# Experts of two MoE layers put in order of their token counts on the chip, the small ones four abreast

## The chip, the cores and the metric
The kernel runs on one core of a Trainium2 chip. The metric is device time in microseconds (us), from the launch's start to the end of its last instruction. TensorE is written PE (its weight loads PEld), VectorE DVE, ScalarE ACT, GpSimd POOL, SyncE SP. SP issues nearly all DMAs. Everything is float32 or a pair of fp32r values, high and low half, unless said otherwise.

## The reference
Two transformer blocks over 512 tokens of width 1024. Each block ends in a two-level mixture of experts (MoE) with 32 experts, in 4 groups of 8. A token takes its best group, and in that the best two experts, so 1024 assignments go to 32 experts, 32 on average. The experts of block 1 have a hidden width F of 512, those of block 2 one of 256. In short:

```
grp_p, grp_idx = top_k(softmax(x @ w_grp + b_grp), 1)
in_grp = (x @ w_exp + b_exp).reshape(T, 4, 8)[arange(T), grp_idx[:, 0]]
top_l, top_i = top_k(in_grp, 2)
comb = grp_p * softmax(top_l)
y = zeros(T, 1024)
for (t, e, w) in assignments:          # e = grp_idx * 8 + top_i
    y[t] += w * ((silu(x[t] @ w1[e]) * (x[t] @ w3[e])) @ w2[e])
```

## The kernel before
The MoE layers (MoE1 in block 1, MoE2 in block 2) are two objects of one class, `Moe`. The router (`Route`) leaves in `rt` the rank of each token within its expert (L404; 0 where the token isn't the expert's) and in `wl` its weight, as high and low half (L433, L434). The 32 experts form 16 pairs. A pair has 128 slots, 64 for each expert; two pairs are gathered together as a unit, so there are 8 units.

For a unit, `onehot` (L451) compares `rt` with the slot numbers, and `gather_k` (L457) multiplies the normalized tokens (stationary, 128x128) by that matrix: 64 matmuls of 256 columns bring the tokens of 256 slots to the partitions. `slot_weights` (L464) brings their weights. For a pair, `gateup` multiplies gate and up (L643): the slots of each expert are a stationary of 64 columns, the weights are moved in 512 columns, and the experts j = 0 and 1 of the pair alternate, in the two halves of the array. `spread` (L631) transposes the one-hot matrix. `finish` transposes the product (L662), multiplies by the down weights (L673, again two abreast), scales by the modulation row and splits into halves (ACT `yh`, POOL `yl`), and sends the rows back to the tokens with 16 matmuls of 512 columns (`back`, L688), which DVE adds to the sum (L694). The down part of pair p runs amid the gate and up part of pair p+1 (`mid`).

Weights are streamed by SP (L566) into slots of 1 MB that rotate: 15 in MoE1, 8 in MoE2. A slot is free when the matmuls that read it are done. In MoE1 a pair is 12 tiles: 8 gate and up tiles as 128 partitions x 4 rows x 512 (each row of 2 KB a piece of its own in DRAM), 4 down tiles as 128 x 2 x 1024 (4 KB). In MoE2 it is 4 gate-up tiles, of two DMAs each, in pieces of 1 KB, and 2 down tiles. The list `jobs` sets SP's order: gate tiles of p, down tiles of p-1, up tiles of p. 15 tiles of MoE1 are sent for before its first matmul.

An expert with more than 64 tokens would need a further pass: `passes` (L519 to L524) works out their number `nex` from the largest rank, every engine reads it (L717), and a loop (L720) runs so often. In the runs shown it is 0. The order of instructions on each engine comes from a scheduler that interleaves them by its own estimate of times; around the router it is written by hand.

Of the kernel before, what the change touches and what calls it, by code (L numbers as in the profile page):

```python
# [20 lines left out]
P = 128  # L21
T = 512
TB = 4
# [4 lines left out]
NPAIR = 16  # L28
# [30 lines left out]
C_N = 664  # L59
# [9 lines left out]
def _constants():  # L69
# [14 lines left out]
    c[:, C_THR + 7] = 1e9  # L84
    e = np.zeros((33, RL), np.float32)
# [12 lines left out]


# [54 lines left out]
def body(tc, I, out, dbg=None):  # L154
# [15 lines left out]
    with top:  # L170
# [179 lines left out]
        class Route:  # L350
# [57 lines left out]

            def weights(self, a, b):
# [39 lines left out]
        def onehot(d, pm, n):  # L449
            w = [P, pm.shape[1], n, CAP]  # L450
            V.tensor_tensor(d.rearrange("p t (e s) -> p t e s", e=n), pm.unsqueeze(3).to_broadcast(w),  # L451
                            cst[:, C_IO64:C_IO64 + CAP].unsqueeze(1).unsqueeze(1).to_broadcast(w), op=ALU.is_equal)
# [7 lines left out]
        def slot_weights(d, wlx, o, n, pl):  # L460
            wsl = tl(pl, [P, 2], tag="wsl", bufs=2)
            for pp in range(n // 2):
                for tb in range(TB):
                    PE.matmul(o[:, 4 * pp:4 * pp + 4], d[:, tb, P * pp:P * pp + P],  # L464
                              wlx[:, tb, 2 * pp:2 * pp + 2, :].rearrange("p e l -> p (e l)"),
                              start=tb == 0, stop=tb == TB - 1)
            for j in range(2):
                hf = slice(CAP * j, CAP * j + CAP)
                V.tensor_reduce(wsl[hf, 0:n // 2], o[hf, 0:2 * n].rearrange("p (a j l) -> p a j l", j=2, l=2)[:, :, j, :],
                                axis=AX.X, op=ALU.add)  # L470
            return wsl
# [24 lines left out]
        class Lead:  # L496
# [18 lines left out]
            def passes(self, bank):  # L515
                pm = tl(rp, [P, 1], tag="pm", bufs=1)
                th = tl(rp, [1, 8], tag="th", bufs=1)
                o = bank("tr")
                yield lambda: V.tensor_reduce(pm, rt.rearrange("p t e -> p (t e)"), axis=AX.X, op=ALU.max)  # L519
                PE.transpose(o[0:1, 0:P], pm, ident)  # L520
                yield lambda: V.tensor_reduce(pm[0:1], o[0:1, 0:P], axis=AX.X, op=ALU.max)
                yield lambda: V.tensor_scalar(th, cst[0:1, C_THR:C_THR + 8], pm[0:1], None, op0=ALU.is_le)
                yield lambda: V.tensor_reduce(pm[0:1], th, axis=AX.X, op=ALU.add)
                yield lambda: V.tensor_copy(nex[0:1, 0:1], pm[0:1])  # L524

            def slots(self, bank):
                return self.d, self.xT, slot_weights(self.d, wl, bank("tr"), 4, rp)


        class Moe:  # L530
            def __init__(self, w1, w3, w2, F, wpool, npre, more=0):
                self.w = [w.rearrange("(q b) d f -> q b d f", b=4) for w in (w1, w3, w2)]
                self.F, self.FC = F, F // P
                self.wpool, self.more = wpool, more
                js = [self.thunks(self.static(p_), wpool, p_) for p_ in range(NPAIR)]
                nd = self.FC
                self.upto = []
                self.jobs = []
                for p_ in range(NPAIR):
                    self.jobs += js[p_][0:4]  # L540
                    if p_:
                        self.jobs += js[p_ - 1][-nd:]
                    self.jobs += js[p_][4:-nd]
                    self.upto.append(len(self.jobs))
                self.jobs += js[-1][-nd:]
# [4 lines left out]
            def static(self, p_):  # L550
                return lambda i, j: self.w[i][p_ // 2, 2 * (p_ % 2) + j]
# [6 lines left out]
            def thunks(self, get, wpool, key, half=1):  # L558
                def kview(ap):
                    return ap.rearrange("(k p) f -> p k f", p=P)  # L560

# [9 lines left out]
                kg, kd = 4 // half, max(2 // half, 1)  # L571
                if F == 512:
                    for i, nm in enumerate("gu"):
                        for s_ in range(KC // kg):
                            for j in range(2):
                                out_.append(mk(nm, j, s_, [P, kg, F], [
                                    (lambda t: t, lambda i=i, j=j, s_=s_: kview(get(i, j))[:, kg * s_:kg * s_ + kg, :])]))
                else:
                    for s_ in range(KC // kg):
                        for j in range(2):  # L580
                            out_.append(mk("gu", j, s_, [P, kg, 2, F], [
                                (lambda t, i=i: t[:, :, i, :], lambda i=i, j=j, s_=s_: kview(get(i, j))[:, kg * s_:kg * s_ + kg, :])
                                for i in range(2)]))
                if half > 1:
                    for s_ in range(self.FC):
                        for n in range(2):
                            for j in range(2):
# [3 lines left out]
                for s_ in range(self.FC // kd):  # L591
                    for j in range(2):
# [4 lines left out]
            def run(self, hs, acc, grow, side, lead, keep, area):  # L597
# [3 lines left out]
                with es:  # L601
# [8 lines left out]
                    def gather(pmx, wlx, pl, n, ar):  # L610
                        w = n * CAP
                        d = ar[0]()
                        onehot(d, pmx, n)
                        xT = ar[1]()
# [6 lines left out]
                        return d, xT, slot_weights(d, wlx, bk("m"), n, rp if n == 4 else pl)  # L621

                    def gateup(ga, pp, ws, key, half=1, last=False, mid=None):
# [14 lines left out]
                        for i in range(F // 256):  # L638
                            for k in range(KC):
                                for j in range(2):  # L640
# [11 lines left out]
                    def finish(st, ws, key, half=1, le=G, last=False):  # L652
# [15 lines left out]
                        for k in range(FC):  # L668
                            for n in range(2):
                                for j in range(2):  # L670
                                    w = ws[key, "d", j, (k, n)][:, 0] if half > 1 else \
                                        ws[key, "d", j, k // 2][:, k % 2, 512 * n:512 * n + 512]
                                    PE.matmul(os_[n][CAP * j:CAP * j + CAP], gT[:, k, CAP * j:CAP * j + CAP], w,  # L673
# [40 lines left out]
                    with ExitStack() as ls:  # L714
# [4 lines left out]
                        V.tensor_copy(cur, rt)  # L719
                        with tc.For_i(0, n, 1) as it:  # L720
# [8 lines left out]
                            with tc.For_i(0, NQUAD, 1) as iq:  # L729
# [6 lines left out]
                                for pp in range(2):  # L736
                                    gl = gather(pm4[:, :, 2 * pp:2 * pp + 2], wl4[:, :, 2 * pp:2 * pp + 2, :], lw, 2, local(lw, 2 * CAP))
# [19 lines left out]
                    held = NPAIR - (1 if big_ else NE2)  # L757

                    def down(st, p_):
                        cm = finish(st, self.tiles, p_, le=G if p_ + 1 < NPAIR else V, last=p_ >= held)  # L760
# [5 lines left out]
                    for p_ in range(NPAIR):  # L766
# [1365 lines left out]
```

## Time and profile before

| | |
|---|---|
| median of 3 runs | 2041.03 us (2038.62 to 2044.96) |
| profiled execution | 2044.01 us, span 2042.2 us |
| MoE1 (stretch 854 to 1409 us) | 555 us, PE busy 534.34 us, DMA 344 GB/s |
| between the MoEs (1409 to 1687) | 278 us, PE busy 242.60 us, DMA 91 GB/s |
| MoE2 (1687 to 2021) | 334 us, PE busy 332.18 us, DMA 277 GB/s |

The stretches are read off the timeline, from the first gate matmul of a MoE to its last combine. Matmuls are pipelined, so a group's busy time counts overlap once within the group, and several groups can be busy at once; the time from the start of one matmul to the start of the next says what a matmul costs PE. A `SPq` row is a DMA issue and the time it waited, not the transfer.

### The profile page before, as it was taken

To read this page: it belongs to the slowest core of one execution; us is meant where nothing else is said; L and a number is where in the kernel's file an instruction comes from. 1 tells how busy PE (TensorE), PEld (TensorE's weight loads), DVE (VectorE), ACT (ScalarE), POOL (GpSimd) and SP (SyncE) were. 2 spreads that over 40 slices of the span, in tenths; PEclk is the share of its full clock that TensorE was granted. 3 is DMA by queue.
4 is the path that set the end of the run, shared out by engine and by line. 5 is a ranking of instruction groups with operands and counts; after the bars stand their busy time and mean duration, and the time that the engine had idled before them with its cause. 6 is when DMAs were issued, how large, how long until landed. Compare 5 with 4: busy or idle time off the path is not lost. (4 is left out here: it accounts for less than half of the span.)

```text
span 2042.2 us, 25610 instructions
## 1 busy us (share of the span) xinstructions
PE 1877.7 (92%) x10105; PEld 1231.2 (60%) x10105; DVE 939.5 (46%) x1667; ACT 652.4 (32%) x1076; POOL 463.6 (23%) x372
## 2 busy tenths in 40 slices
PE   6889988889999999699999999997899989999997
PEld 4767777777788889444444434433775774445443
DVE  4784748445454778522213221225644561333336
ACT  3677567211467622110101010012435431111113
POOL 5333324433354422200000000103312010111113
PEclk9999989989999999799999999998999989999999
DMA  9541725696522154599999999983221438987883
GB/s 317 171 147 63 253 63 180 224 285 192 171 91 76 55 182 161 212 392 395 356 346 360 369 346 345 366 315 104 65 75 45 145 125 289 313 305 255 281 289 123
DMA packets 268447, 451.62 MB, mean 221 GB/s; under 512 B 19486, under 2 KB 154314, under 8 KB 268316
## 3 DMA queue, kind: packets, MB, share of 16 engines
q1 hardware_dynamic: 267996, 449.80, 63.5%
q8 instruction: 84, 1.38, 0.3%
q14 instruction: 47, 0.39, 0.1%
q0 software_dynamic: 320, 0.07, 0.0%
HBM read 445.54 MB, written 8.61 MB: 222 GB/s over the span
## 5 line engine op out<-in xcount | busy, mean ns | idle before, releaser
L216 POOL TENSOR_TENSOR wlo<-raw,whi 128x2048 fp32r<-128x2048 f32 (+2 forms) x72 | 220.6, 3078 | 353.7 <-ACT whi L213 330.2
L643 PE MATMUL gu<-w,xT 128*64 128x512 f32 x1024 | 277.8, 614 | 5.2 <-issue 5.2
L237 PE MATMUL pj<-hi,whi 128*128 128x512 f32 (+1 forms) x544 | 222.5, 409 | 13.8 <-DVE bsig L1210 7.7
L238 PE MATMUL pj<-lo,whi 128*128 128x512 f32 (+1 forms) x544 | 220.7, 406 | 2.3 <-DVE lo L959 2.3
L239 PE MATMUL pj<-hi,wlo 128*128 128x512 f32 (+1 forms) x544 | 220.1, 406 | 0.7 <-POOL wlo L216 0.4
L643 PEld LDWEIGHTS gu<-w,xT 128*64 128x64 f32 x1024 | 78.9, 140 | 147.6 <-issue 144.7
L216 POOL TENSOR_TENSOR yl<-gy,yh 128x512 fp32r<-128x512 f32 x30 | 38.3, 1277 | 515.9 <-ACT yh L213 515.9
L694 DVE TENSOR_TENSOR acc<-acc,y 128x512 f32<-128x512 f32 x120 | 79.2, 684 | 143.9 <-PE y L688 142.9
L694 DVE TENSOR_TENSOR acc<-acc,c 128x512 f32<-128x512 f32 x112 | 75.6, 685 | 149.5 <-PE c L688 149.1
L643 PE MATMUL gu<-w,clo 128*64 128x512 f32 x512 | 137.9, 613 | 5.4 <-issue 5.4
L836 DVE SCALAR_TENSOR_TENSOR adas<-adar,cact,adas 128x1024 f32<-128x1024 f32 x70 | 123.5, 1775 | 39.0 <-DMA adar<-in_w_ada_dram 27.3
L213 ACT CAST whi<-raw 128x2048 fp32r<-128x2048 f32 (+2 forms) x82 | 104.0, 1299 | 117.3 <-PE pj L238 77.1
L237 PEld LDWEIGHTS pj<-hi,whi 128*128 128x128 f32 (+1 forms) x544 | 105.0, 193 | 39.5 <-DVE bsig L1210 8.2
L673 PE MATMUL y<-w,gy 128*64 128x512 f32 x512 | 122.1, 606 | 1.0 <-ACT gy L667 0.8
L238 PEld LDWEIGHTS pj<-lo,whi 128*128 128x128 f32 (+1 forms) x544 | 105.4, 194 | 26.1 <-DVE lo L959 2.9
L239 PEld LDWEIGHTS pj<-hi,wlo 128*128 128x128 f32 (+1 forms) x544 | 105.1, 193 | 26.3 <-issue 1.8
L683 DVE TENSOR_TENSOR gy<-y,g 128x512 f32<-128x512 f32 x31 | 21.4, 691 | 197.7 <-PE y L673 116.4
L239 PE MATMUL pj<-whi,lo 128*128 128x256 f32 (+1 forms) x368 | 108.1, 294 | 2.3 <-DVE lo L216 1.9
L238 PE MATMUL pj<-wlo,hi 128*128 128x256 f32 (+1 forms) x368 | 107.7, 293 | 1.4 <-POOL wlo L216 1.4
L237 PE MATMUL pj<-whi,hi 128*128 128x256 f32 (+1 forms) x368 | 108.3, 294 | 0.0
L209 ACT ACT_TABLE_LOAD x82 | 105.2, 1283 | 8.5 <-DVEq L720 6.3
L216 POOL TENSOR_TENSOR yl<-yt,yh 128x512 fp32r<-128x512 f32 x28 | 36.7, 1313 | 307.9 <-ACT yh L213 236.1
(557 smaller groups left out, 3735.3 us busy)
## 6 DMA issues: line engine op xcount, KB each, us to landing
w<-in_exp_w_dram SPq DMA_DIRECT2D x192, 1024.0 KB
raw<-in_w_in_dram SPq DMA_DIRECT2D x38, 1024.0 KB
w<-in_w_expert_gate_dram SPq DMA_DIRECT2D x64, 512.0 KB
w<-in_w_expert_up_dram SPq DMA_DIRECT2D x64, 512.0 KB
w<-in_w_expert_down_dram SPq DMA_DIRECT2D x32, 1024.0 KB
adar<-in_w_ada_dram SPq DMA_DIRECT2D x48, 512.0 KB
adar<-in_ada_w_dram SPq DMA_DIRECT2D x32, 512.0 KB
raw<-in_ada_w_dram SPq DMA_DIRECT2D x16, 512.0 KB
```

The lines of the kernel that those rows point to most:

```text
L209: S.activation(out_, in_, fn, bias=zero_c[:in_.shape[0]] if bias is None else bias, scale=scale, **kw)
L213: S.copy(hi, src)
L216: (le or V).tensor_tensor(lo, src, f(hi), op=ALU.subtract)
L237: PE.matmul(o, ah, bh, start=first, stop=False)
L238: PE.matmul(o, ah, bl, start=False, stop=False)
L239: PE.matmul(o, al, bh, start=False, stop=last)
L643: PE.matmul(gu[i][CAP * j:CAP * j + CAP], xT[:, k, c0:c0 + CAP], w if big_ else w.rearrange("p i f -> p (i f)"), start=k == 0, stop=k == K ...
L673: PE.matmul(os_[n][CAP * j:CAP * j + CAP], gT[:, k, CAP * j:CAP * j + CAP], w, start=k == 0, stop=k == FC - 1)
L683: V.tensor_tensor(yt, os_[n], grow[:, sl], op=ALU.mult)
L694: V.tensor_add(acc[:, tb, sl], acc[:, tb, sl], o)
L836: V.scalar_tensor_tensor(sm_[:, cs], r, ck, sm_[:, cs], op0=ALU.mult, op1=ALU.add)
```

## The change
- `sort` takes the place of `passes`: it counts the tokens of each expert by 8 + 8 small matmuls, sets the experts 0 to 3 first and all others by falling count (`pos` is an expert's place), and takes `nex` from the ranks less the places' sizes. `permute` (called when the first pair is under way) brings `rt` and `wl` into that order by transposes and small matmuls and writes the list `eo`: which expert stands at which place.
- 20 places have 64 slots and form 10 pairs (`p`); 12 places have 32 slots and form 3 quads (`q`): four experts in the four quarters of the array, 32 columns each. There are 13 groups in 7 units, in the order p p, p q, p p, p q, p p, p q, p. The last unit's gather has 128 columns.
- The weights of the 28 experts behind the first four are addressed by a register, which SP loads from `eo` (L630, once for each expert).
- A gate or up tile takes two neighbouring rows of DRAM to a partition, pieces of 4 KB in MoE1 and of 2 KB in MoE2 (`rows2`). To match, the gather's stationary takes every second column of the tokens.

By the reference's routing no expert has more than 52 tokens in block 1 and 57 in block 2, and the twelve last places hold at most 29 and 27.

```
-NPAIR = 16
+NS = 4
+N64 = 20
+UNITS = (("p", "p"), ("p", "q"), ("p", "p"), ("p", "q"), ("p", "p"), ("p", "q"), ("p",))
...
+    e = np.arange(NE)
+    c[:, C_KR:C_KR + NE] = np.where(e < NS, 1e6, 0.0) - e
+    c[0:NE, C_KC] = np.where(e < NS, 1e6, 0.0) - e
+    c[0:NE, C_EC] = e
...
+            def sort(self):
+                def t_(shape, tag, dt=F32):
+                    return tl(rp, shape, dt, tag="s_" + tag, bufs=1)
+                o = self.bank("tr")
+                for t2 in range(TB):
+                    PE.matmul(o[:, 0:NE], tri[:, P:2 * P], self.rb[:, t2, :], start=t2 == 0, stop=t2 == TB - 1)
+                for t2 in range(TB):
+                    PE.matmul(o[0:NE, NE:NE + 4], self.rb[:, t2, :], tri[:, P:P + 4], start=t2 == 0, stop=t2 == TB - 1)
+                u = tl(rp, [P, P], tag="r_t4", bufs=1)
+                kr, capx, dg = u[0:NE, 0:NE], u[:, NE:2 * NE], u[0:NE, 2 * NE:2 * NE + NE // 2].bitcast(BF16)
+                self.oh, self.capx, self.eo = kr, capx, u[0:1, 3 * NE:4 * NE].bitcast(I32)
+                sm = t_([NE, 12], "sm")
+                kc, c32, pm, th = sm[:, 0:1], sm[:, 1:2], sm[0:1, 3:4], sm[0:1, 4:12]
+                self.pos = sm[:, 2:3]
+                yield lambda: V.scalar_tensor_tensor(kr, o[0:NE, 0:NE], float(CAP), cst[0:NE, C_KR:C_KR + NE], op0=ALU.mult, op1=ALU.add)
+                yield lambda: V.scalar_tensor_tensor(kc, o[0:NE, NE:NE + 1], float(CAP), cst[0:NE, C_KC:C_KC + 1],
+                                                     op0=ALU.mult, op1=ALU.add)
+                yield lambda: V.tensor_scalar(kr, kr, kc, None, op0=ALU.is_ge)
+                yield lambda: V.tensor_reduce(self.pos, kr, axis=AX.X, op=ALU.add)
+                yield lambda: V.tensor_scalar(c32, self.pos, N64 + 0.5, 32.0, op0=ALU.is_le, op1=ALU.mult)
+                yield lambda: V.tensor_scalar(dg, ident[0:NE, 0:NE], c32, None, op0=ALU.mult)
+                PE.matmul(o[:, 64:64 + NE], tri[0:NE, P:2 * P], dg, start=True, stop=True)
+                yield lambda: V.tensor_scalar(capx, o[:, 64:64 + NE], -32.0, None, op0=ALU.add)
+                yield lambda: V.tensor_tensor(kr[0:1], o[0:1, 0:NE], capx[0:1], op=ALU.subtract)
+                yield lambda: V.tensor_reduce(pm, kr[0:1], axis=AX.X, op=ALU.max)
+                yield lambda: V.tensor_scalar(th, cst[0:1, C_THR:C_THR + 8], pm, None, op0=ALU.is_le)
+                yield lambda: V.tensor_reduce(pm, th, axis=AX.X, op=ALU.add)
+                yield lambda: V.tensor_copy(nex[0:1, 0:1], pm)
...
+            def permute(self, bk, rT, wT):
+                oh, eo = self.oh, self.eo
+                V.tensor_scalar(oh, cst[0:NE, C_IO64:C_IO64 + NE], self.pos, None, op0=ALU.is_equal)
+                for src, dst in ((rt, rT), (self.t["wv"], wT)):
+                    o = bk("m")
+                    for tb in range(TB):
+                        PE.transpose(o[0:NE, tb * P:tb * P + P], src[:, tb, :], ident)
+                    S.copy(dst, o[0:NE, :])
+                o = bk("m")
+                PE.matmul(o[0:1, 256:256 + NE], cst[0:NE, C_EC:C_EC + 1], oh, start=True, stop=True)
+                for i, src in enumerate((rT, wT)):
+                    for tb in range(TB):
+                        PE.matmul(o[:, P * i + NE * tb:P * i + NE * tb + NE], src[:, tb * P:tb * P + P], oh, start=True, stop=True)
+                V.tensor_copy(eo, o[0:1, 256:256 + NE])
+                V.tensor_copy(rt, o[:, 0:P].rearrange("p (t e) -> p t e", t=TB))
+                wp_ = o[:, P:2 * P].rearrange("p (t e) -> p t e", t=TB)
+                V.tensor_copy(wl[:, :, :, 0], wp_)
+                V.tensor_tensor(wl[:, :, :, 1], wp_, f(wl[:, :, :, 0]), op=ALU.subtract)
...
-                    PE.matmul(o, h[:, tb, k * P:(k + 1) * P], d[:, tb, :],
+                    PE.matmul(o, h[:, tb, 2 * P * (k // 2):2 * P * (k // 2 + 1)].rearrange("p (d r) -> p r d", r=2)[:, k % 2], d[:, tb, :],
...
+                self.units = _groups()
+                self.groups = [g for u in self.units for g in u]
+                js = [self.thunks(self.at(*g), wpool, p_, ne=g[1]) for p_, g in enumerate(self.groups)]
+                first = [2 * g[1] for g in self.groups]
+                nd = [self.FC // 2 * g[1] for g in self.groups]
...
-            def static(self, p_):
-                return lambda i, j: self.w[i][p_ // 2, 2 * (p_ % 2) + j]
+            def at(self, e0, ne, cap):
+                regs = {}
+                def get(i, j):
+                    if e0 < NS:
+                        return self.we[i][e0 + j]
+                    if j not in regs:
+                        regs[j] = nc.values_load(self.route.eo[0:1, e0 + j:e0 + j + 1], engines=[SY.engine], min_val=0, max_val=NE - 1,
+                                                 skip_runtime_bounds_check_because="places are a permutation of the experts")
+                    return self.we[i][bass.ds(regs[j], 1)].rearrange("a d f -> (a d) f")
...
+                def rows2(ap, k0, n):
+                    v = ap.rearrange("(a p r) f -> p a r f", p=P, r=2)
+                    if n == 1:
+                        return v[:, k0 // 2, k0 % 2, :].unsqueeze(1).unsqueeze(1)
+                    return v[:, k0 // 2:(k0 + n) // 2]
...
+                            for j in range(ne):
+                                out_.append(mk(nm, j, s_, [P, ka, kr, F], [
+                                    (lambda t: t, lambda i=i, j=j, s_=s_: rows2(get(i, j), kg * s_, kg))]))
...
-                                for j in range(2):
-                                    c0 = P * pp + CAP * j
-                                    w = ws[key, "gu"[i] if big_ else "gu", j, k // kg][:, k % kg]
-                                    PE.matmul(gu[i][CAP * j:CAP * j + CAP], xT[:, k, c0:c0 + CAP],
-                                              w if big_ else w.rearrange("p i f -> p (i f)"), start=k == 0, stop=k == KC - 1)
+                                for j in range(ne):
+                                    cap = P // ne
+                                    c0 = P * pp + cap * j
+                                    w = ws[key, "gu"[i] if big_ else "gu", j, k // kg][:, k % kg // 2]
+                                    w = w[:, k % min(kg, 2)] if big_ else w[:, :, k % min(kg, 2), :]
+                                    o = gu[i][cap * j:cap * j + cap]
+                                    PE.matmul(o if big_ else o.rearrange("p (i f) -> p i f", i=2), xT[:, k, c0:c0 + cap], w,
+                                              start=k == 0, stop=k == KC - 1)
                             if i == 0 and mid:
                                 mid()
...
-                    for p_ in range(NPAIR):
-                        q = p_ // 2
-                        if p_ % 2 == 0 and q:
-                            ga[q] = gather(rt[:, :, 4 * q:4 * q + 4], wl[:, :, 4 * q:4 * q + 4, :], None, 4, area(q))
-                        self.emit(self.upto[p_])
-                        st = gateup(ga[q], p_ % 2, self.tiles, p_, last=p_ >= held,
-                                    mid=p_ and (lambda st=st, p_=p_: down(st, p_ - 1)))
+                    p_ = 0
+                    for q, gs in enumerate(self.units):
+                        for pp, (e0, ne, cap) in enumerate(gs):
+                            if p_ == 1:
+                                route.permute(bk, *[tl(mpx[0], [P, 512], tag=t, bufs=1 if big_ else NY2)[0:NE] for t in ("yh", "yl")])
+                            if pp == 0 and q:
+                                ga[q] = gather(rt, wl, None, gs, area(q))
+                            self.emit(self.upto[p_])
+                            st = gateup(ga[q], pp, self.tiles, p_, last=p_ >= held, ne=ne,
+                                        mid=p_ and (lambda st=st, p_=p_: down(st, p_ - 1)))
+                            p_ += 1
                     self.emit(len(self.jobs))
-                    down(st, NPAIR - 1)
+                    down(st, ng - 1)```

On PE in MoE1, a stretch of gate matmuls: before the gate of a pair (`gu_8107`; `w_` are its weight tiles, `xT` the gathered tokens), then its down transposes.

```order
L643 MATMUL gu_8107<-w_8084,xT_7997 64x512
L643 MATMUL gu_8107<-w_8082,xT_7997 64x512
L643 MATMUL gu_8107<-w_8084,xT_7997 64x512
L643 MATMUL gu_8107<-w_8086,xT_7997 64x512
L643 MATMUL gu_8107<-w_8088,xT_7997 64x512
L643 MATMUL gu_8107<-w_8086,xT_7997 64x512
L643 MATMUL gu_8107<-w_8088,xT_7997 64x512
```

And now the gate of the first quad (`gu_8329`), behind the down matmuls of the pair before it.

```order
L768 MATMUL y_8188<-w_8153,gy_8189 64x512
L737 MATMUL gu_8329<-w_8286,xT_8044 32x512
L737 MATMUL gu_8329<-w_8291,xT_8044 32x512
L737 MATMUL gu_8329<-w_8276,xT_8044 32x512
L737 MATMUL gu_8329<-w_8281,xT_8044 32x512
L737 MATMUL gu_8329<-w_8286,xT_8044 32x512
L737 MATMUL gu_8329<-w_8291,xT_8044 32x512
L737 MATMUL gu_8329<-w_8276,xT_8044 32x512
```

Two weight tiles alternated; now four do, with 32 slots each.

On SP at MoE1's start, the weight tiles behind the 15 that are sent for ahead; before:

```order
L566 DMA w_7878<-in_exp_w_dram 128x4x512
L566 DMA w_7880<-in_exp_w_dram 128x4x512
L566 DMA w_8082<-in_exp_w_dram 128x4x512
L566 DMA w_8084<-in_exp_w_dram 128x4x512
L566 DMA w_8086<-in_exp_w_dram 128x4x512
L566 DMA w_8088<-in_exp_w_dram 128x4x512
```

And now (`r_t_1149_7098` holds the list `eo`):

```order
L655 DMA w_7924<-in_exp_w_dram 128x2x1024
L655 DMA w_7926<-in_exp_w_dram 128x2x1024
L655 DMA w_8147<-in_exp_w_dram 128x2x1024
L655 DMA w_8149<-in_exp_w_dram 128x2x1024
L655 DMA w_8151<-in_exp_w_dram 128x2x1024
L630 TENSOR_LOAD r_t_1149_7098
L655 ISA
L655 DMA w_8133<-in_exp_w_dram 128x2x1024
L630 TENSOR_LOAD r_t_1149_7098
L655 ISA
L655 DMA w_8138<-in_exp_w_dram 128x2x1024
```

Three down tiles of the second pair (`w_8147`, `w_8149`, `w_8151`) moved ahead of the first tile of a sorted expert, and a register load stands between.

On PE, where `eo` is made; before, the up matmuls of the second pair (`gu_7884`) ran straight into the down matmuls of the first:

```order
L643 MATMUL gu_7884<-w_7880,xT_7125 64x512
L643 MATMUL gu_7884<-w_7878,xT_7125 64x512
L643 MATMUL gu_7884<-w_7880,xT_7125 64x512
L673 MATMUL y_7906<-w_7173,gy_7908 64x512
L673 MATMUL y_7906<-w_7868,gy_7908 64x512
```

And now (`m_7894` and `m_7900` are `permute`'s):

```order
L473 MATMUL m_7894<-cst_67,r_wv_6339 32x128 x4
L737 MATMUL gu_7930<-w_7926,xT_7140 64x512
L737 MATMUL gu_7930<-w_7924,xT_7140 64x512
L737 MATMUL gu_7930<-w_7926,xT_7140 64x512
L737 MATMUL gu_7930<-w_7924,xT_7140 64x512
L737 MATMUL gu_7930<-w_7926,xT_7140 64x512
L476 MATMUL m_7900<-r_t_1149_7098,cst_67 1x32
L479 MATMUL m_7900<-r_t_1149_7098,yh_7885 128x32 x4
L479 MATMUL m_7900<-r_t_1149_7098,yl_7886 128x32 x4
L756 MATMUL m_7947<-cst_67,sgm_7841 128x128 x4
L768 MATMUL y_7952<-w_7190,gy_7954 64x512
```

The matmul that makes `eo` (L476) stands behind all up matmuls of the second pair, and so behind the landing of `w_7924` and `w_7926`.

## Rows read from the trace of the kernel before

**Rows 1.** The page: busy time, share of the span, instructions of PE.
```profile
PE 1877.7 (92%) x10105; PEld 1231.2 (60%) x10105; DVE 939.5 (46%) x1667; ACT 652.4 (32%) x1076; POOL 463.6 (23%) x372
```
**Rows 2.** Windows: stretch and its us, busy of each engine, PEclk, DMA share, GB/s.
```profile
854.00:1409.00 555.00, 534.34 (x2408) 236.82 (x2408) 130.81 (x202) 55.92 (x92) 38.30 (x30) 0.97 0.93 344
1687.00:2021.00 334.00, 332.18 (x1584) 162.33 (x1584) 116.28 (x187) 46.50 (x93) 39.25 (x30) 0.99 0.81 277
900.00:1100.00 200.00, 195.62 (x918) 91.49 (x918) 50.30 (x80) 21.88 (x36) 15.34 (x12) 0.97 0.99 371
```
**Rows 3.** Waits of SP in MoE1 (859 to 1372): us in total, times, longest.
```profile
SPq L566 <- PE gu L643: 275.1, 85, 11.0
SPq L566 <- PE y L673: 97.6, 31, 13.2
```
**Rows 4.** Waits of SP in MoE2 (1694 to 1997).
```profile
SPq L566 <- PE gu L643: 127.8, 38, 9.8
```
**Rows 5.** Line L566: issue ns (min/median/max), first and last start; who waited for it.
```profile
L566 SPq DMA_DIRECT2D w<-in_exp_w_dram x192: 367/368/4225, 761.8 to 1371.1; - x192
...
  PEld gu L643: 0.2, 1
```
**Rows 6.** PE by line, MoE1 (854 to 1409): count, busy us, mean ns, idle before.
```profile
L643 PE MATMUL gu<-w,xT 128*64 128x512 f32 x1024 | 277.8, 614 | 5.2 <-issue 5.2
L673 PE MATMUL y<-w,gy 128*64 128x512 f32 x512 | 122.1, 606 | 1.0 <-ACT gy L667 0.8 <-issue 0.2
L688 PE MATMUL y<-yh,DT 128*128 128x512 f32 x120 | 54.7, 466 | 10.8 <-ACT yh L213 9.3 <-DVE gy L683 1.3
```
**Rows 7.** The same for MoE2 (1687 to 2021).
```profile
L643 PE MATMUL gu<-w,clo 128*64 128x512 f32 x512 | 137.9, 613 | 5.4 <-issue 5.4
L673 PE MATMUL y<-w,sgm 128*64 128x512 f32 x256 | 65.4, 601 | 0.0
```
**Rows 8.** Timeline of PE at MoE1's start: start, us, instructions, idle before.
```profile
854.16 15.49 PE L643 MATMUL gu<-w,xT 128*64 128x512 f32 x64 [5.20 <-issue]
869.59 0.66 PE L631 MATMUL m<-identr,D 128*128 128x128 f32 x4
870.17 7.09 PE L643 MATMUL gu<-w,xT 128*64 128x512 f32 x32
```
**Rows 9.** Timeline of PE at MoE1's end.
```profile
1399.95 0.50 PE L688 MATMUL y<-yh,DT 128*128 128x512 f32 x1
...
1400.89 0.40 PE L688 MATMUL y<-yl,DT 128*128 128x512 f32 x1
1401.51 7.11 PE L673 MATMUL y<-w,gy 128*64 128x512 f32 x32 [0.23 <-issue]
```
**Rows 10.** Timeline of PE in a gather of MoE2.
```profile
1713.14 0.28 PE L457 MATMUL gu<-chi,hi 128*128 128x256 f32 x1
...
1714.09 0.28 PE L457 MATMUL gu<-chi,hi 128*128 128x256 f32 x1
```
**Rows 11.** Windows where one piece size moves alone: 2 KB, 4 KB, 1 KB.
```profile
866.00:874.00 8.00, 8.00 (x40) 2.85 (x38) 0.75 (x1) 0.58 (x1) 0.00 (x0) 1.00 1.05 387
1125.00:1135.00 10.00, 8.50 (x39) 2.63 (x35) 0.69 (x1) 1.30 (x2) 0.38 (x1) 1.00 1.01 402
1702.00:1708.00 6.00, 6.00 (x39) 3.46 (x36) 0.55 (x2) 0.75 (x2) 0.00 (x0) 1.00 1.09 352
```
**Rows 12.** Timeline of PE, an earlier stage with stationaries of 32 columns.
```profile
199.37 1.06 PE L840 MATMUL tr<-adas,ones 128*32 128x512 f32 x8
```
**Rows 13.** Timelines of DVE at `passes` and of SP at the first freed slot.
```profile
843.27 0.28 DVE L519 TENSOR_REDUCE pm<-rt 128x1 f32<-128x128 f32 x1
845.73 0.13 DVE L524 CAST nex<-pm 1x1 int32<-1x1 f32 x1
...
859.38 4.35 SPq L566 DMA_DIRECT2D w<-in_exp_w_dram  x4
```
**Rows 14.** Line L717, SP's reading of `nex`: ns (min/median/max).
```profile
L717 SPq TENSOR_LOAD <-nex x2: 466/475/484, 845.9 to 1680.1; - x2
...
L717 SPq FUSED_REGOPS  x2: 162/174/186, 846.4 to 1680.6; - x2
```

More of the change, by code (lines that the diff above doesn't have):

```diff
@@ L58 @@
 C_THR = 656
-C_N = 664
+C_KR = 664
+C_KC = 696
+C_EC = 697
+C_N = 698
 def _bucket(dist):
@@ L97, in _ap, with _groups @@
     return bass.AP(tensor=t.tensor, offset=t.offset + off, ap=[list(t.ap[0])] + [list(d) for d in dims])
+def _groups():
+    n64, n32, units = 0, N64, []
+    for u in UNITS:
+        gs = []
+        for g in u:
+            if g == "p":
+                gs.append((n64, 2, 64))
+                n64 += 2
+            else:
+                gs.append((n32, 4, 32))
+                n32 += 4
+        units.append(gs)
+    assert n64 == N64 and n32 == NE
+    return units
 class _Slots:
@@ L513, in end @@
                     place(self.xT, 2 * k2, 2, self.o[k2], k2, S)
[L515 to L524, printed above, removed]
             def slots(self, bank):
-                return self.d, self.xT, slot_weights(self.d, wl, bank("tr"), 4, rp)
+                return self.d, self.xT, slot_weights(self.d, wl, bank("tr"), [(0, 2, CAP), (2, 2, CAP)], rp)
         class Moe:
@@ L586, in thunks @@
                         for n in range(2):
-                            for j in range(2):
+                            for j in range(ne):
                                 out_.append(mk("d", j, (s_, n), [P, 1, 512], [
@@ L591, in thunks @@
                 for s_ in range(self.FC // kd):
-                    for j in range(2):
+                    for j in range(ne):
                         out_.append(mk("d", j, s_, [P, kd, D], [
@@ L595, in thunks, with run @@
                 return out_
-            def run(self, hs, acc, grow, side, lead, keep, area):
+            def run(self, hs, acc, grow, side, lead, keep, area, route):
                 F, FC = self.F, self.FC
@@ L608, in run, with gather @@
                     mpx = [None]
[L610 to L614, printed above, removed]
+                    def gather(pmx, wlx, pl, gs, ar):
+                        w = P * len(gs)
+                        d = ar[0]()[:, :, 0:w]
+                        for pp, (e0, ne, cap) in enumerate(gs):
+                            onehot(d[:, :, P * pp:P * pp + P], pmx[:, :, e0:e0 + ne], ne, cap)
+                        xT = ar[1]()[:, :, 0:w]
                         kb = 512 // w
@@ L650, in gateup, with finish @@
                         return spread if last else spread(), sg
-                    def finish(st, ws, key, half=1, le=G, last=False):
+                    def finish(st, ws, key, half=1, le=G, last=False, ne=2):
                         DT, sg = st
@@ L669, in finish @@
                             for n in range(2):
[L670 removed]
+                                for j in range(ne):
+                                    cap = P // ne
                                     w = ws[key, "d", j, (k, n)][:, 0] if half > 1 else \
                                         ws[key, "d", j, k // 2][:, k % 2, 512 * n:512 * n + 512]
[L673 removed]
+                                    PE.matmul(os_[n][cap * j:cap * j + cap], gT[:, k, cap * j:cap * j + cap], w,
                                               start=k == 0, stop=k == FC - 1)
@@ L756, in run @@
                     late = [None]
-                    held = NPAIR - (1 if big_ else NE2)
+                    self.route = route
+                    ng = len(self.groups)
+                    held = ng - (1 if big_ else NE2)
                     def down(st, p_):
-                        cm = finish(st, self.tiles, p_, le=G if p_ + 1 < NPAIR else V, last=p_ >= held)
+                        cm = finish(st, self.tiles, p_, le=G if p_ + 1 < ng else V, last=p_ >= held, ne=self.groups[p_][1])
                         if late[0]:
@@ L1659, in body @@
             ld.feed(3, 4, 0, 2)
-            weave(ld.passes(bank), r1.weights(0, 4))
+            weave(r1.sort(), r1.weights(0, 4))
             ld.feed(3, 4, 2)
@@ L2061, in body @@
                 ld.feed(3, 4, 0, 2)
-                weave(ld.passes(bank), r2.weights(3, 4))
+                weave(r2.sort(), r2.weights(3, 4))
                 ld.feed(3, 4, 2)
```

62 lines of the change are left out of this document (31 added, 31 removed).

## The prediction
> **What bounds the kernel now.** I read the page first: PE is busy for 92% of the span [rows 1], so time is won on PE or not at all, unless another resource stands close behind. The windows by stage show where. In MoE1 PE is busy 534.3 of 555 us, in MoE2 332.2 of 334 [rows 2]; the change touches these two stages and the 4 us of routing ahead of each. Third come the waits, from both sides. SP, which issues the weights, waited 275.1 + 97.6 us in MoE1 for gate, up and down matmuls to free a slot [rows 3], and 127.8 us for gate and up in MoE2 [rows 4]; the other way round gate and up matmuls waited for weights 0.2 us in all [rows 5]. So PE sets the pace in both and the weights follow it. But in MoE1 they follow closely: DMA share 0.93 over the stage, 0.99 over 200 us in its middle, at 371 GB/s [rows 2]. In MoE2 it is 0.81. Whatever PE saves in MoE1 is capped by the transfers; in MoE2 there is more room. That is the frame of the sum.
>
> **PE, per group.** A round of two abreast takes 7.09 us / 16 = 0.443 us (32 matmuls, rows 8); 7.11 / 16 on the down side [rows 9]. A MoE1 pair has 1024/16 = 64 gate and up matmuls [rows 6], 32 rounds = 14.2 us; 32 down matmuls, 16 rounds = 7.1; 16 sends back at (1400.89 - 1399.95)/3 = 0.31 us, 5.0 [rows 9]; spread and transposes 0.66 each, 1.3 [rows 8]. Sum 27.6 us; 16 of them, 442. A gather's matmuls start 0.95/8 = 0.12 us apart [rows 10]: 64 are 7.7 us, seven 54. Together 496 of the 534 busy; the other 38 are restarts of broken runs and small matmuls.
> A quad takes four experts through one group, if its four matmuls share a round. That this works rests on [rows 12]: eight matmuls with stationaries of 32 columns in 1.06 us, two rounds of four; by twos they would need four rounds, 1.7 us. So six pairs become three quads, MoE1 loses three groups: 3 x 27.6 = 83, and one gather of seven, 7.7. `permute` adds eight transposes (two times 0.66) and nine small matmuls, 3 us with the breaks in the runs. PE in MoE1: -88.
> In MoE2 a group has 16 rounds of gate-up (7.1) and 8 of down (3.6) by counts of [rows 7]; with back and spread as above 17, while (332.2 - 54)/16 = 17.4 counts everything. I take 16, since the restarts don't all go. 3 x 16 + 7.7 - 3: -53, to about 280.
>
> **DMA in MoE1.** 192 tiles, 15 sent ahead; 177 x 1.0486 MB = 185.6 MB from 859.4 [rows 13] to about 1378 (last issue at 1371, rows 5). Alone, 2 KB pieces run at 387 GB/s, 4 KB at 402 [rows 11], so `rows2` lifts two thirds of the bytes by 4%. At 402 without a gap it is 462 us. The 200 us at share 0.99 made 371, where the mix of 387 and 402 would give 392, that is 95%; then 486. I take 475. A cycle p p p q costs PE 4 x 34 = 136 us (534/16 = 33.4 for a group with its share of a gather), the DMA 3 x 12 + 24 = 60 tiles, 60 x 1.0486/0.402 = 156. DMA therefore becomes the bound in MoE1, and 15 slots (39 us of transfer) hold the 9 us of lead that three pairs can give to a quad.
> Two delays add to it. The last tile's consumers: half the down matmuls (3.6), scaling, sends back (5.0): 12 us. And SP stops at its register load until `eo` is there. That is behind the second pair's up matmuls, in the order of PE, and behind it the whole queue of weights waits; three static down tiles (8 us) stand ahead of it. PE passes that point about two groups after 854, near 886; I reckon 5 us without transfer (0 if the tiles ahead cover it, 15 if those wait for slots).
> `sort`: `passes` ran from 843.27 to 845.73 [rows 13], and all engines wait for `nex` before the MoE. 13 DVE steps for 5, at 0.13 to 0.28 us and interleaved with the weights' steps, and a matmul amid them, less the transpose that goes: +2.5 us a layer (0 to 5).
> End of MoE1: 859.4 + 2.5 + 5 + 475 + 12 = 1354, for 1408.6 now: -54.
>
> By the Trainium skill ("DMA: Bandwidth & Descriptors", "Where 436 GB/s comes from") the memory side, at about 358 GB/s a core, binds transfers from HBM to SBUF. This trace disagrees: 371 over 200 us, 402 over 10. By the rule MoE1's transfers would take 185.6/0.358 = 518 us, its end would come at 1397, 12 us sooner than now, and the whole at about 2001; it speaks against any large gain there. Rival E is its like, from rows.
>
> **DMA in MoE2.** A pair is 6.3 MB: at 352 for 1 KB pieces [rows 11], and 402 for down tiles, 17.3 us. In 2 KB pieces (387) it is 16.1, a quad 32.1. Cycle: PE 3 x 20 + 20 = 80 (332/16 with the gather), DMA 80.3. They are even, so neither is hidden: with eight slots, fewer than a quad's 12 tiles, quads run at the DMA's pace and pairs at PE's. If nothing of that is evened out PE loses 12 us for each quad, if all is, none. I take half, 18 of 36: -53 + 18 = -35, and with 2.5 for `sort` and 2 at the register load -30.
>
> **What costs nothing, and its cover.** The strided stationary of the gather: no row shows a strided load. If it were twice as slow to load, 384 loads a layer cost up to 25 us on PE; in MoE1 the DMA covers that now, in MoE2 nothing does. If it is free, 0. I take 0, since a gather matmul lasts 0.28 us and the next starts after 0.12 [rows 10], so loads already run beside matmuls. SP's register work: 28 loads and 168 register DMAs in MoE1. The nearest rows, 0.48 + 0.17 us for reading a register and 0.37 for an issue [rows 14, 5], against a tile each 2.6 us: covered. The unpaid part is rival D. The stage between the MoEs doesn't change.
>
> **Sum** on the profiled execution: 2044.0 - 54 - 30 = 1960. The median is 3 us lower: 1957.
>
> **Rivals.**
> A, the forecast (0.52): DMA binds MoE1, half of the unevenness costs MoE2. Own range 1930 to 1985.
> B (0.20): no lead carries over, since eight DMAs in flight and slots in rotation only let the stream run one group ahead; each group costs the larger of PE and DMA. MoE1: 10 x 34 + 3 x 62.6 = 528, with 12 of tail 540, -15; MoE2: 10 x 20 + 3 x 32.1 = 296, with 14 of lead and tail 310, -22. Sum with 5 for `sort`: 2044 - 32 - 3 = 2009. For: quads need twice a pair's weights at once. Against: SP's waits show that the stream runs to the slots' end already.
> C (0.17): everything evens out; MoE1 ends at 859.4 + 462 + 12 = 1333, -75, MoE2 -53, 5 back: 2044 - 123 - 3 = 1918. For: the 0.97 clock and few gaps. Against: the 0.95 of [rows 2].
> D (0.06), slower: a DMA with its address in a register costs SP more than a plain one, and SP, which issues everything in order, becomes the bound. 168 such DMAs in MoE1, 140 in MoE2 (two for each gate-up tile). At 3 us each: MoE1 504 + 20, -30; MoE2 420 + 15 = 435, +103; 2044 + 73 - 3 = 2114. Above 2.6 us each it outweighs all gains. For: no row of the trace has one. Against: the 1 us of [rows 14, 5].
> E (0.03): the long-run rate is set by the memory side, not by the pieces, and stays at the stage's 344 GB/s [rows 2]. MoE1 ends at 859.4 + 7.5 + 185.6/0.344 + 12 = 1419, +10; in MoE2 a quad takes 12.6/0.344 = 36.6, so 10 x 20 + 3 x 36.6 + 14 = 324 without any lead, 280 with all of it, half 302, with 4.5 of delays -25: 2044 - 15 - 3 = 2026. Against: the 371 [rows 2].
> F (0.02), it doesn't do what it says: quads run by twos. Then only the back, spread, gather and 4 KB pieces are won, some 3 x 6.3 + 7.7 - 3 = 24 a layer: 1994. [Rows 12] speak against. Extra passes by small places are shut out by the counts (29 and 27 for 32).
>
> **Chances and range.** 0.3%, 6 us, is what a measurement tells from no change. Faster by more: A, B, C, E, F less a little for mishaps: 0.92; within: 0.02; slower: D, 0.06. Range 1912 to 2011, which takes in C and B.
>
> **What would show it.** In MoE1 a DMA share of 0.98 or more at about 385 to 400 GB/s, SP waiting far less than 373 us for PE, and `gu` waiting for weights tens of us, above all in quads. In MoE2 such waits of 0 to 36 us, in quads alone. 16 quad matmuls in about 1.8 us. I am wrong if SP's issue of a register DMA takes over 2 us, if PE stays above 95% busy in MoE1 (C or cheaper DMA), or if gathers lengthen beyond 0.12 us a step.

## The result, and the profile after

The changed kernel took 1965.37 us (median of 4 runs, 1961.20 to 1968.27) beside 2039.82 (2035.43 to 2044.96) before: ratio 0.963, 95% interval 0.960 to 0.966. The forecast was 1957. Its sum fits, but two of its terms don't: MoE1 won more than it said, MoE2 almost nothing, and for another reason than the one it gave. That the sum fits is luck in part: the two errors have opposite signs.

The windows of the kernel after (stretch and its us, busy of PE, PEld, DVE, ACT, POOL, then PEclk, DMA share, GB/s): MoE1, MoE2, and 350 us inside MoE1.
```profile
855.00:1340.00 485.00, 466.14 (x2284) 194.62 (x2286) 108.16 (x187) 46.09 (x76) 30.75 (x24) 0.98 0.99 393
...
1619.00:1945.00 326.00, 314.51 (x1479) 147.86 (x1480) 102.47 (x182) 40.75 (x78) 31.30 (x24) 0.98 0.78 284
...
960.00:1310.00 350.00, 338.19 (x1686) 142.57 (x1683) 79.20 (x133) 32.79 (x54) 23.02 (x18) 0.99 1.03 409
```
MoE1 went from 555 to 485 us [rows 2], MoE2 from 334 to 326. From the start of the first gate matmul to the start of the last down matmul it is 553.9 to 484.6 and 331.2 to 324.4; the stage between gave 1.5, what follows MoE2's last down matmul 4.1 (why is open), and MoE1 starts 1.4 later. That makes the 80.3 us between the two spans. In MoE1 the transfers run at 409 GB/s for 350 us. PE is busy there for 96% of the time all the same, so the windows alone don't tell which of the two binds; the experiments below say that it is the transfers. In MoE2 the DMA share fell from 0.81 to 0.78. PE's busy time, between the same two matmuls, fell from 330.8 to 313.0 us, and its idle time rose from 0.5 to 11.5, in many waits of at most 2.6 us.

SP's waits in MoE1 of the kernel after (us, times, longest), for [rows 3]:
```profile
SPq L655 <- PE gu L737: 96.8, 41, 8.4
SPq L655 <- PE y L783: 61.8, 39, 4.0
SPq L655 <- PE y L768: 47.9, 22, 13.7
...
SPq L630 <- DVE r_t L480: 9.4, 1, 9.4
```
Gate, up and down matmuls held SP for 373 us before and for 145 now; sends back (L783) hold it for 62, which were 13. The register load waited 9.4 us for the list. The issues themselves (ns, min/median/max) and who waited for the weights, for [rows 5, 14]:
```profile
L655 SPq FUSED_REGOPS  x308: 37/43/56, 890.7 to 1932.6; - x154
...
L655 SPq DMA_DIRECT2D w<-in_exp_w_dram x192: 367/2152/4265, 761.4 to 1316.6; - x192
L655 SPq MOVE w<-in_exp_w_dram x168: 29/29/38, 890.7 to 1316.5; - x168
...
L655 SPq DMA_DIRECT2D w<-in_w_expert_down_dram x32: 368/373/453, 1625.0 to 1932.9; - x32
...
  PEld y L768: 13.7, 13
...
  PEld gu L737: 0.2, 1
```
```profile
L630 SPq TENSOR_LOAD <-r_t x56: 262/272/301, 890.3 to 1895.9; - x56
```
A register address costs one operation of 43 ns and one move of 29 ns on SP (308 addresses in the two layers), a register load 272 ns. The issue itself is as short as before in MoE2 (373 ns), but in MoE1 its median is 2152 ns. Gate matmuls still don't wait for weights.

So why did MoE2 win so little? PE's groups there, by shape (count, busy us, mean ns), for [rows 7]; first the kernel after:
```profile
L737 PE MATMUL gu<-w,clo 128*64 128x512 f32 x320 | 88.8, 616 | 5.2 <-issue 5.2
L768 PE MATMUL y<-w,sgm 128*64 128x512 f32 x160 | 49.4, 618 | 2.6 <-DMA w<-in_w_expert_down_dram 2.6
...
L737 PE MATMUL gu<-w,clo 128*32 128x512 f32 x192 | 38.5, 597 | 0.0
...
L768 PE MATMUL y<-w,sgm 128*32 128x512 f32 x96 | 22.3, 598 | 0.5 <-ACT sgm L761 0.5
```
192 matmuls, four abreast, are 48 rounds, 21 us at 0.443 us each; they took 38.5. 96 are 24 rounds, 11 us; they took 22.3. The timeline of PE shows how:
```profile
1687.22 3.62 PE L737 MATMUL gu<-w,clo 128*32 128x512 f32 x26
...
1691.79 1.93 PE L768 MATMUL y<-w,sgm 128*64 128x512 f32 x4
...
1695.52 3.65 PE L768 MATMUL y<-w,sgm 128*64 128x512 f32 x12
```
Four down matmuls take 1.93 us, one after another, each a round of its own; twelve take what sixteen took [rows 9: 32 in 7.11]. That is what matmuls of one expert side by side, without their partners, would do. I counted rounds in the traces (matmuls of one group that start within 0.1 us of each other are one):

| gate, up and down rounds | MoE1 | least possible | MoE2 | least possible |
|---|---|---|---|---|
| before | 854 | 768 | 428 | 384 |
| after | 755 | 624 | 422 | 312 |

In MoE2 the quads should have saved 72 rounds of the least possible; 66 of them were lost again. Of the 422 rounds the quads have 128, where 72 are the least possible, and the pairs 294 for 240: both are broken.

### The profile page after: what moved, and what is told of

It is laid out like the page before. It is cut to its first block, busy times and chain, and to the rows that moved or that the text cites. A ratio compares the mean times of both kernels' runs of the same rounds, so it can differ in the third digit from the quotient of the medians.

```text
span 1961.9 us, 25761 instructions
## 1 busy us (share of the span) xinstructions
PE 1797.7 (92%) x9883; PEld 1174.0 (60%) x9883; DVE 895.3 (46%) x1659; ACT 636.5 (32%) x1044; POOL 446.6 (23%) x360
## 5 line engine op out<-in xcount | busy, mean ns | idle before, releaser
L737 PE MATMUL gu<-w,xT 128*64 128x512 f32 (+1 forms) x1024 | 242.3, 610 | 5.8 <-issue 5.8
L264 PE MATMUL pj<-hi,whi 128*128 128x512 f32 (+1 forms) x544 | 224.1, 412 | 13.2 <-DVE bsig L1311 7.8
L737 PEld LDWEIGHTS gu<-w,xT 128*64 128x64 f32 (+1 forms) x1024 | 62.9, 129 | 129.4 <-issue 126.8
L243 POOL TENSOR_TENSOR yl<-gy,yh 128x512 fp32r<-128x512 f32 x24 | 30.8, 1281 | 457.4 <-ACT yh L240 394.8
L737 PE MATMUL gu<-w,clo 128*64 128x512 f32 (+1 forms) x512 | 127.3, 609 | 5.2 <-issue 5.2
L768 PE MATMUL y<-w,gy 128*64 128x512 f32 (+1 forms) x512 | 109.9, 602 | 5.1 <-DMA w<-in_exp_w_dram 4.2
L789 DVE TENSOR_TENSOR acc<-acc,y 128x512 f32<-128x512 f32 x96 | 63.4, 685 | 111.0 <-PE y L783 110.5
L789 DVE TENSOR_TENSOR acc<-acc,c 128x512 f32<-128x512 f32 x88 | 58.2, 685 | 109.5 <-PE c L783 105.3
L778 DVE TENSOR_TENSOR gy<-y,g 128x512 f32<-128x512 f32 x25 | 17.3, 691 | 183.5 <-PE y L768 139.4
L243 POOL TENSOR_TENSOR yl<-yt,yh 128x512 fp32r<-128x512 f32 x22 | 28.8, 1317 | 281.7 <-ACT yh L240 220.4
```

The lines of the kernel that those rows point to most:

```text
L243: (le or V).tensor_tensor(lo, src, f(hi), op=ALU.subtract)
L264: PE.matmul(o, ah, bh, start=first, stop=False)
L737: PE.matmul(o if big_ else o.rearrange("p (i f) -> p i f", i=2), xT[:, k, c0:c0 + cap], w, start=k == 0, stop=k == KC - 1)
L768: PE.matmul(os_[n][cap * j:cap * j + cap], gT[:, k, cap * j:cap * j + cap], w, start=k == 0, stop=k == FC - 1)
L789: V.tensor_add(acc[:, tb, sl], acc[:, tb, sl], o)
```

## Experiments

Times are medians; each ratio is to the kernel before, run beside it on the same chip. "MoE1 +5" means the time from the start of the first gate matmul to that of the last down matmul, in the one profiled run of each kernel.

**Rounds held together (after_lock, before_lock).** Edges tell the scheduler that the first matmul of a tile group waits for the weights of all its experts and that the others follow in program order. The two kinds of edge weren't tried apart.
```
+            def together(self, mm, sent):
...
+                for x in sent:
+                    tc.add_manual_dep(mm[0], x.name, info(mybir.DependencyClass.Sync), reason="round")
+                for a, b in zip(mm, mm[1:]):
+                    tc.add_manual_dep(b, a.name, info(mybir.DependencyClass.NoSync), reason="round")
```


> The changed kernel, with edges that hold the matmuls of one round together: the gate, up and down matmuls of a tile group wait for the weights of all experts of the group, and follow each other in program order. In the changed kernel's trace MoE2 has 422 rounds of gate-up and down matmuls (before 428), where 312 would do. Theory (PE bounds MoE2, and the order breaks its rounds): some 100 rounds of 0.45 us go, PE falls by 45 us there until the transfers bind, MoE2 gets 25 to 35 us shorter, MoE1 0 to 5; total 1930 to 1942. Rival (the quads starve for weights in MoE2, as my forecast had it): no change beyond 6 us, 1959 to 1971.

1922.54 us, ratio 0.941 (0.938 to 0.944). MoE2 -39.8 (100 rounds less), MoE1 -2.3. The same groups of MoE2 in after_lock:
```profile
L745 PE MATMUL gu<-w,clo 128*64 128x512 f32 x320 | 80.4, 613 | 5.6 <-issue 5.6
...
L780 PE MATMUL y<-w,sgm 128*64 128x512 f32 x158 | 38.3, 629 | 5.9 <-DMA w<-in_w_expert_down_dram 5.9
...
L745 PE MATMUL gu<-w,clo 128*32 128x512 f32 x192 | 21.8, 595 | 0.5 <-issue 0.5
...
L780 PE MATMUL y<-w,sgm 128*32 128x512 f32 x96 | 12.6, 673 | 0.3 <-DMA w<-in_w_expert_down_dram 0.3
```
The quads now take 21.8 and 12.6 us, the 48 and 24 rounds. And in the timeline, beside the rows above:
```profile
1682.38 3.64 PE L745 MATMUL gu<-w,clo 128*32 128x512 f32 x32
...
1688.40 3.65 PE L780 MATMUL y<-w,sgm 128*64 128x512 f32 x16
```
The windows of MoE1 and MoE2:
```profile
856.00:1339.00 483.00, 435.40 (x2286) 188.03 (x2286) 107.61 (x187) 46.04 (x76) 30.64 (x24) 0.95 1.00 395
1618.00:1902.00 284.00, 267.94 (x1474) 138.35 (x1472) 100.35 (x179) 39.93 (x76) 31.28 (x24) 0.96 0.88 326
```
The theory holds, and the starving quads, the forecast's explanation, fall: once PE had less to do, the transfers followed (284 to 326 GB/s over MoE2). In MoE1 PE's busy time fell as well, by 31 us, and the time by 2: there the transfers bind, and the broken rounds had only filled PE's waits. This version beats both kernels.

> The kernel before with the same edges. Its MoE1 has 853 rounds where 768 would do, its MoE2 428 where 384 would. Theory: PE bounds both, so MoE1 loses up to 38 us and MoE2 20, MoE1 less where its transfers bind (about 480 us of them); total 1990 to 2005. Rival (broken rounds are only where PE waits for weights anyway): within 6 us of 2040.

2006.62, ratio 0.984 (0.980 to 0.988): MoE1 -27.2 (58 rounds less, 0.47 us each), MoE2 -4.6 (only 8 less; 72 rounds there still hold a single matmul, and 22 of these stand before a send back). The total is 2 us above what the theory allowed: in MoE1 as expected, in MoE2 the edges didn't reach what they were to mend.

**Four abreast taken away (lock_twos).** In after_lock, quarters 0 and 1 run through a tile group, then 2 and 3 (the down loop likewise):
```
-                            for k in range(KC):
-                                for j in range(ne):
+                            for k, j in [(kg * a + b, 2 * c + e) for a in range(KC // kg) for c in range(ne // 2) for b in range(kg) for e in range(2)]:
...
```


> The kernel after_lock, with the four experts of a quad taken in two rounds of two instead of one of four (quarters 0 and 1 for all steps of a tile group, then 2 and 3); sorting, places, groups, gathers and transfers are the same. Theory (four abreast is what wins PE's time): quads cost 21 us more each in MoE1 and 11 in MoE2, 64 and 32 in all; MoE1 has slack on PE (435 busy of 483), so it gets 20 to 35 us longer, MoE2 20 to 32; total 1962 to 1988. Rival (the gain comes from fewer groups, sends back and gathers): within 8 us of 1922.

1935.31, ratio 0.948 (0.945 to 0.951): MoE1 +5, MoE2 +13.6. Between the theory and the rival. The trace tells why: at the change of halves the last matmuls of one and the first of the next still shared rounds, so only 64 and 34 rounds came back, not 144 and 72. MoE2's 34 at 0.40 us fit the price of a round; MoE1's 64 lengthened PE's busy time by 23 us and moved the stage by 5, because transfers bind it. The profiled run was 10.7 us above the median, and its two stages add up to 18.5 us where the medians give 13, so the 13.6 may be too high by some us.

So the price of a round in MoE2 is 0.40 us (100 less: -39.8; 34 more: +13.6). From before to after only 6 rounds went, 2.4 us of the 6.8. PE's busy time fell by 17.8 us in all, with sends back and gathers, and 11.0 us of that came back as idle time.

**The quads taken away (after_pairs).**
```
-N64 = 20
+N64 = 32
+UNITS = (("p", "p"),) * 8
```


> The changed kernel with 32 places of 64 slots: sort, permute, register addresses and the pieces stay, but there are 16 pairs and 8 gathers as before, and no quad. Theory (all that is won comes from the quads, the rest of the change costs a little): 1.5 us for sort and 3 for permute in each layer and the wait for the list, 3 to 12 us slower than before, 2044 to 2053. Rival (sorting or the pieces bring something by themselves): under 2035.

2064.33, ratio 1.011 (1.008 to 1.014): 24 us slower than before, twice what I allowed. In the profiled run MoE1 starts 1.6 later and takes 6.3 longer, MoE2 8.7. So all that comes with the quads (sorting, list, registers, pieces) costs some 20 us, and the quads, with the groups and the gather that they save, win near 100. Of the 8.7 in MoE2, 6 rounds more than before are 2.4 at 0.40 us; which part costs the rest stays open.

**The registers taken away (after_fixed).**
```
...
-                    return self.we[i][bass.ds(regs[j], 1)].rearrange("a d f -> (a d) f")
+                    return self.we[i][ORDER[self.F][e0 + j]]
```


> The changed kernel with the order of the experts as constants, so that no register load, no register address and no wait for the list stands in SP's way; sort and permute still run, PE's order is the same. Theory (registers are cheap, the transfers of MoE1 pause only for the list, 9.4 us of SP waiting): 3 to 8 us faster in MoE1, 0 to 3 in MoE2; total 1955 to 1963. Rival (register DMAs slow the stream): 15 us or more, under 1950.

1956.02, ratio 0.957 (0.954 to 0.959): MoE1 -7.2, MoE2 -1.6. Rather the theory; 9 us in all, by SP's issues MoE1's in its first 150 us. But the order of PE isn't the same as was meant: it differs in places, and MoE1 has 744 rounds for 755, so the 7.2 aren't the registers' alone. What the run does settle is the long issue in MoE1, which is there without registers too:
```profile
L654 SPq DMA_DIRECT2D w<-in_exp_w_dram x192: 367/2037/4467, 764.4 to 1312.0; - x192
```
In after_pairs, with registers but with PE as the bound, the median is 373 ns. So the issue is long where the transfers bind, not where an address comes from a register.

**The hole at the list (lock_early, lock_static8).** In lock_early `permute` is called between gate and up of the first pair; in lock_static8 `NS = 8`. The sort also puts those first eight in order of their counts, while the weights of the places 4 to 7 stay those of the experts 4 to 7; so the kernel computes something else than the reference there, with the same amount of work.

> The kernel after_lock, with MoE1's permute called between gate and up of the first pair instead of behind it, so that the list is there before SP reaches the register load (it waited 9.4 us there, and three static tiles stood ahead). Theory (MoE1 is bound by its transfers, and that wait is a hole in them): MoE1 3 to 8 us shorter, total 1914 to 1920. Rival (tiles in flight cover the wait): within 2 us.

1924.32, ratio 0.943 (0.940 to 0.946). SP's wait for the list fell from 9.4 to 3.6 us, MoE1 stayed (+0.6).

> The kernel after_lock, with the first eight experts instead of four left in their own order and at fixed addresses; the list is then first needed for the third pair's successor, eleven tiles later on SP. The twelve last places still hold at most 30 and 28 tokens. Theory (the hole at the list costs MoE1's stream what after_fixed won there, 5 to 7 us): MoE1 3 to 7 us shorter, total 1914 to 1920. Rival (as lock_early showed, slots held by PE take the place of that wait): within 3 us of 1922.

1922.12, ratio 0.942 (0.939 to 0.945); MoE1 +1.1. Both times the rival: the 25th tile is issued 7 and 18 us sooner, but the 37th is issued at 918.1 in lock_early and 916.8 in lock_static8, for 918.1 in after_lock (first gates at 857.5, 854.4 and 856.4). PE frees slots no sooner. What after_fixed won there beyond this wait is not settled; its SP order differs too.

**The pieces (after_pieces, before_pieces, before_lock_pieces, lock_pieces, lock_rows4).** Pieces of before in the changed kernel, or the other way round; of after_pieces:
```
-                                    (lambda t: t, lambda i=i, j=j, s_=s_: rows2(get(i, j), kg * s_, kg))]))
+                                    (lambda t: t, lambda i=i, j=j, s_=s_: kview(get(i, j))[:, kg * s_:kg * s_ + kg, :])]))
...
```


> The changed kernel with the pieces of before (2 KB in MoE1, 1 KB in MoE2) and the gather's stationary in one run of columns; PE's order is the same. Theory (transfers bind MoE1, PE binds MoE2): MoE1 10 to 15 us longer (387 for 402 GB/s on two thirds of the bytes), MoE2 0 to 5; total 1975 to 1985. Rival (transfers bind MoE2 too): MoE2 15 to 20 us longer as well, 1990 to 2000. Rival (the strided stationary costs PE): MoE2 shorter by 5 to 20.

1979.92, ratio 0.970 (0.966 to 0.974): MoE1 +12.6, MoE2 +3.9, as the theory said. PE's order is the same, yet MoE1 has 788 rounds for 755 (MoE2 418 for 422): where weights come late, waiting for them breaks rounds too.

> The kernel before with the pieces of the changed kernel alone (4 KB in MoE1, 2 KB in MoE2, and the strided stationary of the gather); 16 pairs, no sorting, PE's order the same. Theory (PE bounds both layers before): 0 to 6 us faster, 2035 to 2043. Rival (transfers count before too): MoE1 12 us shorter, MoE2 5, 2023 to 2028. Rival (the strided stationary costs PE): slower by 5 to 40.

2042.58, ratio 1.000 (0.999 to 1.002): nothing, PE bound both layers before.

> The kernel before_lock with those pieces. With its rounds together MoE1 was at a DMA share of 0.97 for 527 us, so theory: transfers bind it there and the pieces give 8 to 14 us in MoE1, 0 to 3 in MoE2; total 1992 to 2000. Rival (PE still binds it): within 4 us of 2006.

2009.21, ratio 0.985 (0.982 to 0.989): the rival. before_lock's DMA share of 0.97 over MoE1 didn't mean that transfers bound it:
```profile
847.00:1374.00 527.00, 507.65 (x2408) 224.96 (x2408) 131.49 (x201) 55.53 (x92) 38.19 (x30) 0.99 0.97 361
```
PE was busy 508 of 527 us, and the rate of 361 says what the share doesn't: with 4 KB pieces it stayed at 363.

> The kernel after_lock with the pieces of before (2 KB in MoE1, 1 KB in MoE2) and the plain gather. Theory (with its rounds together MoE2 is bound by its transfers as MoE1 is): two thirds of 92 MB at 352 instead of 387 GB/s are 16 us, MoE2 10 to 18 us longer, MoE1 12 to 16; total 1944 to 1957. Rival (PE still binds MoE2): MoE2 0 to 4 us longer as in after_pieces, 1934 to 1941.

1939.96, ratio 0.950 (0.947 to 0.952): MoE1 +17.0, MoE2 +1.2. The rival: even in after_lock PE binds MoE2.

> The kernel after_lock with four neighbouring rows to a partition: pieces of 8 KB in MoE1 and 4 KB in MoE2, and the gather's stationary takes every fourth column. Theory (transfers bind MoE2, strided stationaries are free): MoE2 3 to 6 us shorter (402 for 387 GB/s on two thirds), MoE1 0 to 3; total 1914 to 1921. Rival (a stride of four slows the loads of the gather): 384 loads a layer at up to twice 0.12 us, 10 to 45 us longer where PE binds, total over 1926.

1979.07, ratio 0.969 (0.966 to 0.972): 57 us longer than after_lock, MoE2 +44.1, MoE1 +12.5. The rival, and a surprise. The gather's weight loads (ns) with every fourth column, every second (after_lock), and every column (lock_pieces):
```profile
L534 PEld LDWEIGHTS gu<-chi,hi x192: 307/330/334, 1655.5 to 1919.2; 128*128 128x128 f32 x192
```
```profile
L534 PEld LDWEIGHTS gu<-chi,hi x192: 192/197/330, 1641.3 to 1863.2; 128*128 128x128 f32 x192
```
```profile
L534 PEld LDWEIGHTS gu<-chi,hi x192: 186/188/333, 1658.9 to 1879.9; 128*128 128x128 f32 x192
```
A gather matmul then starts every 0.23 us instead of 0.12 to 0.13; 384 times 0.1 us, an estimate, is most of MoE2's loss.

## Why the prediction was right, and where not

- **DMA becomes the bound in MoE1: right**, but two of the forecast's own signs say the opposite. PE stayed above 95% busy (466 of 485 us), and gate matmuls waited 0.2 us for weights, not tens. Both mislead here: after_lock took 31 us of PE's busy time away and MoE1 hardly moved, after_pieces took from the rate and MoE1 grew by 12.6. In size, I took 475 us from 859.4 for the transfers, 5 for the register load and 12 for the tail. By the packets in the trace those 185.6 MB had moved at about 1332, 471 us behind the first freed slot (861.05) with the pause at the list, at 409 GB/s for most of it; the tail took 9. MoE1 ended 68 us sooner, not 54. The 409 also rule out rival E. The Trainium skill ("DMA: Bandwidth & Descriptors", "Where 436 GB/s comes from") puts the bound of such transfers at about 358 GB/s a core; this trace disagrees, with 409 for one core alone.
- **PE in MoE2 falls by 53, quads starve and take 18 back: this step failed.** It counted the rounds of the new groups as full (7.1 and 3.6 us a group) and let three groups' worth go, 72 rounds. The runs showed 422 rounds for 428: the rounds were broken, and PE's busy time fell by 17.8 us. The 66 rounds that didn't go are 29 of the 35 us that are missing, at 0.443 us. (In MoE1, too, it fell by 67 us and not by 88, with 99 rounds less and not 144; the transfers covered that.) PE's idle time grew by 11.0, but no quad starved: gate matmuls waited 0.2 us for weights, after_pieces moved MoE2 by 4. So MoE2 won 6.8. With the rounds held together PE's busy time fell by 62 us, its idle time grew by 16, and MoE2 won 47. That this is near the 53 is luck in part: 106 rounds went, 34 of them broken before the change already, which the forecast had not counted. (Its cycle of 80 us for PE takes 332/16 as 20; it is 20.8, so a cycle is 83 and PE and DMA weren't as even as it says.)
- **The sum: luck in part.** MoE1 ended 14 us sooner than forecast, and what comes behind it won 12 us where 30 were forecast.
- **sort +2.5: right.** From `rt` to `nex` it takes 5.5 us (842.27 to 847.77) for 3.0 (842.70 to 845.73), and the first gate starts 1.45 us later.
```profile
847.77 0.13 DVE L464 CAST nex<-s_sm 1x1 int32<-1x1 f32 x1
```
- **The register load, 5 us without transfer: in size right** (share 0.47 from 880 to 892), but shortening SP's wait for the list won nothing in lock_early and lock_static8.
```profile
880.00:892.00 12.00, 10.70 (x60) 4.74 (x56) 1.61 (x5) 1.44 (x3) 0.00 (x0) 1.00 0.47 177
```
- **Registers are cheap (against D): right**, 43 and 29 ns an address. The sign against it, an issue of over 2 us, did come (2152 ns), but it is the transfers' (after_fixed, 2037 ns without registers).
- **Quads share a round (against F): right**, 32 matmuls in 3.64 us in after_lock.
- **The strided stationary at nothing: right for every second column** (197 for 188 ns), only just.
- Of B's and C's prices neither came; C's MoE1 (-75) was nearer than mine.

## What to carry to other kernels

Matmuls that could share the array did so here only where they came one behind another. So count rounds in the order, not matmuls, before working out what a denser packing wins; a scheduler that orders them by its own estimate of times can undo it, and edges within a round gave 43 us here. A high DMA share alone doesn't say that transfers bind, and a busy PE doesn't say that they don't: change the rate, or PE's work, and see.

## What the runs showed of the hardware

- A stationary read at every fourth fp32 column loads in 330 ns, at every second in 197, at each in 188.
- 4 KB pieces moved at 409 GB/s for 350 us on end, above the 402 of the ten microseconds in [rows 11].
- Stationaries of 32 columns in four quarters, with four weight streams, run in rounds of 0.43 to 0.46 us, as two of 64 do (32 matmuls in 3.64 us, 16 in 3.65).
- SP's issue of a DMA took 0.37 us where PE was the bound, and 2.15 us (median) in MoE1 where the transfers were; with fixed addresses 2.04.
